# Row sums of the conditioning in the first block's feed-forward part: halved loads, a quarter of the products on GpSimd and ScalarE, folds a chunk later

## The chip, the cores and the metric

The kernel runs on one core of a Trainium2 chip. The metric is the device time of one execution in microseconds (us); the kernel before takes 3891.92 us, the median of three runs. The core's engines run side by side, each through its own instructions in a fixed order: TensorE (PE, matrix products; PEld is its loading of weights), VectorE (DVE), ScalarE (ACT), GpSimd (POOL). SyncE (SP) issues the loads from memory, one after the other. An instruction that waits for another engine or for a load holds up all that stands behind it on its engine.

## The reference, cut to what matters

The reference runs two network blocks. In the first, each of two layers is steered by numbers that come from a conditioning vector `c` (for 512 latent positions) and `c_ctx` (for 256 context positions): shift, scale and gate of the mixer and of the feed-forward part, six times 1024 numbers.

```
s_lat = silu(c);  s_ctx = silu(c_ctx)
m_lat = split(s_lat @ w_ada[li] + b_ada[li], 6)      # [1024] @ [1024, 6144]
m_ctx = split(s_ctx @ w_ada[li] + b_ada[li], 6)
...
h = rms_norm(x, g_ffn[li]) * (1 + m_lat[4]) + m_lat[3]
x = x + m_lat[5] * conv_ffn(h, ...)                  # up, 3-tap conv, silu * , down
ctx = ctx + m_ctx[5] * conv_ffn(hc, ...)             # in layer 0 only
```

The change touches the products with `w_ada` that are needed late: the last eighth of layer 0 (`m[5]`) and all six parts of layer 1. The kernel computes them while the feed-forward part of layer 0 runs.

## The kernel before

Activations lie feature by feature (128 partitions) with 768 positions in the free direction. A product at full precision is made of three TensorE products of rounded halves: every weight is loaded by SP into a buffer `wraw` (L255), rounded on ACT (`whi`, L262), its rest is taken on DVE (`wlo`, L265), and `mm3` (L271 to L273) multiplies.

`ffn` of layer 0 works in three groups of 8, 7 and 7 chunks (`GROUPS`). In an **up phase** each chunk has two products (m = 0 and 1) into four PSUM banks, which are used in turn; DVE takes them out (`zr`, L633), the convolution goes over ACT (`z`, L642) and DVE (L649), the gate over ACT and DVE (`th`, L653, L654) and GpSimd (`th`, L655), and `split` makes `gh` (ACT, L278) and `gl` (DVE, L279). Since a chunk's product of m = 0 goes into the banks of the chunk before, it can begin only when `zr` of that chunk has been taken out. In the **down phase** behind it eight products f = 0 to 7 run into `psS`, and DVE adds each to the residual (`x`, L591). I call the phases up1, down1, up2, down2, up3 and down3. Behind down3 comes layer 1: its first product (`psP` from `xh`, `xl`), a product for the shift (`psO` from `bh`, `bl`), the mean of squares (`meanrs`, L313), the inverse root on DVE, and `along` (L322), which spreads it.

The generator `rest` (`adarows`) does the conditioning beside this. It has 56 rows, in seven sets of eight; a row is 128 times 1024 numbers of `w_ada`. Before, a row is one load of 512 KB into the only buffer `rada` (L478), and four row sums on DVE (L481, each a product with the conditioning `cr` and a sum, called a dot below; its product is thrown into a `zr` buffer), into `racc`. Behind a set's last row two small TensorE products with `fold` (L486) add the two halves of the partitions, and `biased` (`mc`, `am`) adds the bias. `ffn` draws one row for each up chunk, and one or two for each f (twelve for each down phase). A scheduler then sets the order on every engine by priority, so rows can stand some instructions ahead of or behind the place where the code draws them.

Of the kernel before, what the change touches and what calls it, by code (L numbers as in the profile page):

```python
# [24 lines left out]
F32 = mybir.dt.float32  # L25
F32R = mybir.dt.float32r
I32 = mybir.dt.int32
AF = mybir.ActivationFunctionType
OP = mybir.AluOpType
# [12 lines left out]
GSTART = (0, 8, 15)  # L42
# [44 lines left out]
def drain(steps):  # L87
    for _ in steps:
        pass
# [325 lines left out]
class First(Net):  # L415
# [41 lines left out]
    def adarows(self, wk, sets):  # L457

        nc, I = self.nc, self.I
        cr = wk.tile([128, 2, 512], F32, name="cr")
        src = I["crow"]
        for h in range(2):
            nc.sync.dma_start(cr[64 * h:64 * h + 64], bass.AP(tensor=src.tensor, offset=src.offset + h * 1024, ap=[[0, 64], [1, 1024]]))
        junk = lambda: wk.tile([128, self.wide], F32, name="zr", tag="zr", bufs=2)[:, :512]
        for i in range(2):
            t = junk()
            nc.scalar.activation(t, cr[:, i, :], AF.Tanh, scale=0.5)
            nc.vector.scalar_tensor_tensor(cr[:, i, :], t, 1.0, cr[:, i, :], op0=OP.add, op1=OP.mult)  # L470
        nc.vector.tensor_scalar(cr, cr, 0.5, None, op0=OP.mult)
        fold = wk.tile([128, 64], F32, name="fold")
        nc.vector.tensor_tensor(fold, self.ident[:, 0:64], self.ident[:, 64:128], op=OP.add)
        for l, j0, n in sets:
            acc = wk.tile([128, 2, n, 2], F32, name="racc", tag="racc", bufs=2)
            for j in range(n):
                w = wk.tile([128, 2, 512], F32, name="rada", tag="rada", bufs=1)
                nc.sync.dma_start(w, I["wrow"][l, j0 + j])  # L478
                for b in range(2):
                    for i in range(2):  # L480
                        nc.vector.tensor_tensor_reduce(junk(), w[:, b, :], cr[:, i, :], 1.0, 0.0, OP.mult, OP.add, acc[:, b, j, i:i + 1])  # L481
                if j < n - 1:
                    yield
            ps = self.psT()[:, 0:2 * n]
            for b in range(2):
                nc.tensor.matmul(ps[64 * b:64 * b + 64], lhsT=fold, rhs=acc[:, b].rearrange("p j i -> p (j i)"), start=True, stop=True)  # L486
            self.biased(l, ps.rearrange("p (j i) -> p j i", i=2), j0, n)
            yield

    def run(self):  # L490
        nc, tc, I = self.nc, self.tc, self.I
        self.block("1", NT)
        self.xopen("0", I["x"])
        self.cols = []
        for l in range(DEPTH):
            c = self.cst.tile([128, 245], F32, name=f"cols{l}")
            nc.sync.dma_start(c, I["cols1"][l])
            self.cols.append(c)
        cc = self.cst.tile([128, 8, 2], F32, name="cc")
        nc.sync.dma_start(cc, I["c"])  # L500
        self.sc = self.cst.tile([128, 8, 32], F32, name="sc")
        nc.vector.memset(self.sc, 0.0)
        sc = self.sc[:, :, 0:2]
        nc.scalar.activation(sc, cc, AF.Tanh, scale=0.5)
        nc.vector.scalar_tensor_tensor(sc, sc, 1.0, cc, op0=OP.add, op1=OP.mult)
        nc.vector.tensor_scalar(sc, sc, 0.5, None, op0=OP.mult)
        self.nmx2 = self.cst.tile([128, 8], F32, name="nmx2")
        nc.sync.dma_start(self.nmx2, I["cols2"][0][:, 0:8])
        per = lambda n, k: [self.cst.tile([128, k, 2], F32, name=f"{n}{l}") for l in range(DEPTH)]
        self.mc, self.am, self.af = per("mc", 48), per("am", 8), per("af", 8)  # L510
        self.blk2 = self.cst.tile([128, 2], F32, name="blk2")
        nc.vector.memset(self.blk2, 0.0)
        nc.vector.memset(self.blk2[0:64, 0:1], 1.0)
        nc.vector.memset(self.blk2[64:128, 1:2], 1.0)
        rope = self.cst.tile([128, 2, 128], F32, name="rope")
        nc.sync.dma_start(rope, I["rope1"])
        self.rope = rope
        for l in range(DEPTH):
            self.layer(l, self.mc[l], self.am[l], self.af[l])
# [75 lines left out]
    def ffn(self, E, up, down, cw, nq, same, resid, after):  # L595

        nc, tc = self.nc, self.tc
# [5 lines left out]
        with tc.tile_pool(name="ff", bufs=1, reuse_waits="tile") as wk:  # L603
# [10 lines left out]
            rest = self.adarows(wk, ((0, 40, 8), (1, 8, 8), (1, 0, 8), (1, 16, 8), (1, 24, 8), (1, 32, 8), (1, 40, 8))) if nq > SEQ else iter(())  # L614
            held = 16 if nq > SEQ else 19
            off = 0
            for n, i0 in zip(GROUPS, GSTART):
                gv = []
                for i in range(i0, i0 + n):
                    w = self.chunk(up[i])  # L620
                    z = []
                    for m in range(2):
                        ps = [self.psP()[:, :sz + 2 * (same and j > 0)] for j, (s, sz, o) in enumerate(cuts)]
# [26 lines left out]
                        a = d[:, 1:wide - 1]  # L650
# [6 lines left out]
                    gl = wk.tile([128, wide - 2], F32R, name="gl", tag="gv", bufs=held)  # L657
                    self.split(gh, gl, th)
                    gv.append((gh, gl))
                    next(rest, None)  # L660
                if i0 == GSTART[-1]:
                    N = after(lambda: wk.tile([128, nq], F32, name="nq", tag="th", bufs=2))
                def products(ps, w, j):
# [4 lines left out]

                hold = []
                for f in range(KD):  # L670
                    for _ in range(1 + f % 2):
                        next(rest, None)
                    sz = 128 * n * 128
                    w = self.wload(down[off:off + sz].rearrange("(p a) -> p a", p=128), n, 128)
                    off += sz
                    ps = self.psS()
                    if f == KD - 1 and i0 == GSTART[-1] and N.tail is not None:
                        for s, o in ((0, 0), (256, 512)):
                            for j in range(n):
                                self.mm3(ps[:, o:o + 256], (w[0][:, j, :], w[1][:, j, :]),  # L680
                                         (gv[j][0][:, s:s + 256], gv[j][1][:, s:s + 256]), j == 0, j == n - 1)
                            x = self.xt[f][:, s:s + 256]
                            nc.vector.tensor_tensor(x, x, ps[:, o:o + 256], op=OP.add)
                            N.tail(s)
                        continue
                    for j in range(n - 1 if f < 2 else n):
                        products(ps, w, j)
                    hold.append((f, ps, w))
                    if f == 0:
                        continue  # L690
                    for g, ps, w in hold:
                        if g < 2:
                            products(ps, w, n - 1)
                        resid(g, ps)
                        if i0 == GSTART[-1]:
                            N.step(g)
                    hold = []
            drain(rest)
            self.E = N
            self.banks(("P0", "P1"), ("T0",))  # L700

# [1368 lines left out]
```

## Time and profile before

| | before |
|---|---|
| median of three runs | 3891.92 us (3887.2 to 3895.46) |
| the profiled execution | 3885.17 us |
| its span on the core | 3883.4 us |
| TensorE (PE) busy | 3663.2 us, 94% |
| VectorE (DVE) busy | 2520.5 us, 65% |
| ScalarE (ACT) busy | 1533.8 us, 39% |
| GpSimd (POOL) busy | 553.4 us, 14% |
| row sums L481 | 224 instructions, 175.2 us busy |
| loads of rows L478 | 56, 512 KB each |

The span is the stretch that the profiler recorded; the execution's time is 1.8 us longer. The six phases lie at about 492 to 1073 us of the span, up1 to 630, down1 to 704, up2 to 824, down2 to 887, up3 to 1012 and down3 to 1073. All times below are places in the span or durations.

### The profile page before, as it was taken

Reading aid. Unit: us, or ns where it says so; the run is one execution under the profiler, and the core shown is the slowest. Engines: PE = TensorE matmul, PEld = TensorE weight load, DVE = VectorE, ACT = ScalarE, POOL = GpSimd, SP = SyncE. Lnnn points to the kernel's source line nnn. Section 1 sums busy time; section 2 is a strip of 40 time slices with the busy share of each in tenths; the row PEclk is TensorE's granted clock in tenths of the full one; section 3 lists DMA queues with packets and bytes.
Section 4 is the critical chain, followed back from the end, with each engine's and each line's share of the span. In section 5 each row is a group of like instructions: output and inputs, shape, how many; then the busy total and the mean of one; then the engine's idle time right before and its main releaser. Section 6 shows DMA issues by size and latency. Waiting matters only on the chain. (4 is left out here: it accounts for less than half of the span.)

```text
span 3883.4 us, 58927 instructions
## 1 busy us (share of the span) xinstructions
PE 3663.2 (94%) x23425; PEld 2993.4 (77%) x23425; DVE 2520.5 (65%) x4866; ACT 1533.8 (39%) x2414; POOL 553.4 (14%) x381
## 2 busy tenths in 40 slices
PE   7988999999989899999999899999999988999998
PEld 5866788888887679998876676788887766778886
DVE  5567577778875657557685654656667666456555
ACT  3367432222335644334454322433344533334333
POOL 0022000000222200002112112000021221120002
PEclk9999999999999999999999999999999999999999
DMA  5233233333432133333324336322233343453232
GB/s 180 93 98 109 70 93 114 111 112 110 138 102 58 31 103 90 95 93 116 107 93 132 114 101 226 113 93 94 93 109 109 98 142 101 157 193 96 92 97 77
DMA packets 181987, 422.57 MB, mean 109 GB/s; under 512 B 42320, under 2 KB 62800, under 8 KB 181712
## 3 DMA queue, kind: packets, MB, share of 16 engines
q1 hardware_dynamic: 181712, 418.81, 34.7%
q8 instruction: 184, 3.01, 0.3%
q14 instruction: 91, 0.75, 0.1%
HBM read 373.91 MB, written 44.83 MB: 108 GB/s over the span
## 5 line engine op out<-in xcount | busy, mean ns | idle before, releaser
L262 ACT ACTIVATE whi<-wraw 128x1024 fp32r<-128x1024 f32 (+2 forms) x489 | 510.8, 1046 | 823.1 <-PE psS L272 356.8
L271 PE MATMUL psP<-xh,whi 128*128 128x512 f32 (+1 forms) x2112 | 714.9, 339 | 4.3 <-DVE zr L633 4.3
L273 PE MATMUL psP<-xh,wlo 128*128 128x512 f32 (+1 forms) x2112 | 716.2, 339 | 0.0
L272 PE MATMUL psP<-xl,whi 128*128 128x512 f32 (+1 forms) x2112 | 716.0, 339 | 0.0
L265 DVE TENSOR_TENSOR wlo<-wraw,whi 128x1024 fp32r<-128x1024 f32 (+2 forms) x471 | 575.1, 1223 | 198.2 <-ACT whi L262 190.7
L271 PEld LDWEIGHTS psP<-xh,whi 128*128 128x128 f32 x2112 | 398.7, 189 | 51.8 <-issue 4.5
L272 PEld LDWEIGHTS psP<-xl,whi 128*128 128x128 f32 x2112 | 398.9, 189 | 47.8
L273 PEld LDWEIGHTS psP<-xh,wlo 128*128 128x128 f32 x2112 | 398.8, 189 | 46.6
L655 POOL TENSOR_TENSOR th<-th,z 128x512 f32<-128x512 f32 (+1 forms) x88 | 112.7, 1280 | 1781.5 <-DVE z L649 1686.6
L271 PE MATMUL psS<-gh,whi 128*128 128x512 f32 (+1 forms) x887 | 329.8, 372 | 4.5 <-DVE x L591 3.2
L271 PE MATMUL psP<-hh,whi 128*128 128x512 f32 x800 | 327.8, 410 | 2.0 <-ACT whi L262 1.0
L273 PE MATMUL psS<-gh,wlo 128*128 128x512 f32 (+1 forms) x887 | 329.3, 371 | 0.0
L272 PE MATMUL psS<-gl,whi 128*128 128x512 f32 (+1 forms) x887 | 329.1, 371 | 0.0
L273 PE MATMUL psP<-hh,wlo 128*128 128x512 f32 x800 | 326.5, 409 | 0.7 <-DVE wlo L265 0.7
L272 PE MATMUL psP<-hl,whi 128*128 128x512 f32 x800 | 321.9, 403 | 0.0
L271 PE MATMUL psP<-whi,hh 128*128 128x256 f32 (+1 forms) x944 | 277.0, 294 | 19.0 <-ACT nk L247 4.2
L272 PE MATMUL psP<-wlo,hh 128*128 128x256 f32 (+1 forms) x944 | 273.0, 290 | 5.9 <-DVE wlo L265 5.2
L273 PE MATMUL psP<-whi,hl 128*128 128x256 f32 (+1 forms) x944 | 271.6, 289 | 1.1 <-DVE hl L362 1.1
L271 PEld LDWEIGHTS psP<-whi,hh 128*128 128x128 f32 x944 | 182.8, 194 | 29.5 <-ACT nk L247 4.8
L481 DVE CUSTOM_DVE_ANT_0 zr<-rada,cr 128x512 f32<-128x512 f32 x224 | 175.2, 824 | 45.7 <-DMA rada<-in_wrow_dram 45.1
L271 PEld LDWEIGHTS psS<-gh,whi 128*128 128x128 f32 x887 | 166.7, 188 | 39.8 <-DVE x L591 5.4
L649 DVE SCALAR_TENSOR_TENSOR z<-zr,cols,z 128x770 f32<-128x770 f32 (+3 forms) x176 | 144.3, 820 | 79.6 <-ACT z L642 44.9
(536 smaller groups left out, 6842.1 us busy)
## 6 DMA issues: line engine op xcount, KB each, us to landing
wraw<-in_up_dram SPq DMA_DIRECT2D x176, 512.0 KB
rada<-in_wrow_dram SPq DMA_DIRECT2D x56, 512.0 KB
wraw<-in_down_dram SPq DMA_DIRECT2D x64, 448.0 KB
wraw<-in_gate_dram SPq DMA_DIRECT2D x48, 512.0 KB
wraw<-in_win_dram SPq DMA_DIRECT2D x36, 512.0 KB
wraw<-in_wout_dram SPq DMA_DIRECT2D x32, 512.0 KB
wraw<-in_down_dram SPq DMA_DIRECT2D x32, 512.0 KB
wraw<-in_rwz_dram SPq DMA_DIRECT2D x28, 512.0 KB
```

Source lines behind the costliest of these rows:

```text
L262: self.nc.scalar.activation(hi[:, :n], t[:, :n], AF.Copy)
L265: (self.nc.gpsimd if self.low[self.lows % len(self.low)] == "P" else self.nc.vector).tensor_tensor(lo[:, :n], t[:, :n], hi.bitcast(F32)[:, ...
L271: mm(out, lhsT=l[0], rhs=r[0], start=start, stop=False)
L272: mm(out, lhsT=l[0], rhs=r[1], start=False, stop=False)
L273: mm(out, lhsT=l[1], rhs=r[0], start=False, stop=stop)
L481: nc.vector.tensor_tensor_reduce(junk(), w[:, b, :], cr[:, i, :], 1.0, 0.0, OP.mult, OP.add, acc[:, b, j, i:i + 1])
L649: nc.vector.scalar_tensor_tensor(d[:, o], e[:, q], c(j), d[:, o], op0=OP.mult, op1=OP.add)
L655: nc.gpsimd.tensor_tensor(th, th, z[1], op=OP.mult)
```

## The change

A row is loaded in two halves of 256 KB (`b` = 0 and 1), each a tile `rada` of its own with two buffers in turn, so that the halves `b` = 0 always use one of them and the halves `b` = 1 the other. Three of a row's four dots stay on DVE. The fourth (`b` = 1, `i` = 1) becomes a product on GpSimd, in place in the half's buffer, and a sum on ScalarE (`accum_out`), also in place. `racc` has four buffers and not two. The folds are no longer emitted behind a set: they are collected, and `folded` emits them after the next up chunk's `split` and after the last down phase, into a half of `psS` and not into `T0`. Rows are drawn once for each up chunk (twice at chunks 3 and 12), twice for each f in down1 and down2 (sixteen for each), and not at all in down3. So rows 0 to 8 fall in up1, 9 to 24 in down1, 25 to 32 in up2, 33 to 48 in down2 and 49 to 55 in up3.

```diff
         for l, j0, n in sets:
-            acc = wk.tile([128, 2, n, 2], F32, name="racc", tag="racc", bufs=2)
+            acc = wk.tile([128, 2, n, 2], F32, name="racc", tag="racc", bufs=4)
             for j in range(n):
-                w = wk.tile([128, 2, 512], F32, name="rada", tag="rada", bufs=1)
-                nc.sync.dma_start(w, I["wrow"][l, j0 + j])
                 for b in range(2):
+                    w = wk.tile([128, 512], F32, name="rada", tag="rada", bufs=2)
+                    nc.sync.dma_start(w, I["wrow"][l, j0 + j, :, b, :])
                     for i in range(2):
-                        nc.vector.tensor_tensor_reduce(junk(), w[:, b, :], cr[:, i, :], 1.0, 0.0, OP.mult, OP.add, acc[:, b, j, i:i + 1])
-                if j < n - 1:
-                    yield
-            ps = self.psT()[:, 0:2 * n]
+                        a = acc[:, b, j, i:i + 1]
+                        if b and i:
+                            nc.gpsimd.tensor_tensor(w, w, cr[:, i, :], op=OP.mult)
+                            nc.scalar.activation(w, w, AF.Copy, accum_out=a)
+                        else:
+                            nc.vector.tensor_tensor_reduce(junk(), w, cr[:, i, :], 1.0, 0.0, OP.mult, OP.add, a)
+                if j == n - 1:
+                    self.summed.append((l, j0, n, acc, fold))
+                yield
+
+    def folded(self):
+
+        for l, j0, n, acc, fold in self.summed:
+            ps = self.psS()[:, 0:2 * n]
             for b in range(2):
-                nc.tensor.matmul(ps[64 * b:64 * b + 64], lhsT=fold, rhs=acc[:, b].rearrange("p j i -> p (j i)"), start=True, stop=True)
+                self.nc.tensor.matmul(ps[64 * b:64 * b + 64], lhsT=fold, rhs=acc[:, b].rearrange("p j i -> p (j i)"), start=True, stop=True)
             self.biased(l, ps.rearrange("p (j i) -> p j i", i=2), j0, n)
-            yield
+        self.summed = []
...
                     gv.append((gh, gl))
-                    next(rest, None)
+                    self.folded()
+                    for _ in range(2 if i in (3, 12) else 1):
+                        next(rest, None)
...
                 for f in range(KD):
-                    for _ in range(1 + f % 2):
+                    for _ in range(2 if i0 != GSTART[-1] else 0):
                         next(rest, None)
...
             drain(rest)
+            self.folded()
```

Lines of the changed kernel stand some numbers higher: `zr` L633 is L644 there, `z` L642 is L653, `x` L591 is L602, the dot L481 is L486, and L483 and L484 are the new product and sum.

On SP, in down1, the loads of rows stood between loads of weights (`wraw`), each waiting for the dots of the row before it (DVE) on the only buffer:

```order
151 L478 DMA rada<-in_wrow_dram 128x1024 [waits DMAHW5_49,DVE_49]
152 L255 DMA wraw<-in_up_dram 128x1024 [waits DMAHW3_49,DVE_49]
153 L478 DMA rada<-in_wrow_dram 128x1024 [waits DMAHW7_49,DVE_49]
154 L255 DMA wraw<-in_up_dram 128x1024 [waits DMAHW6_49,DVE_49]
155 L478 DMA rada<-in_wrow_dram 128x1024 [waits DMAHW1_49,DVE_49]
```

In the changed kernel, in down1 and before the weights of the next up phase, they stand so:

```order
189 L479 DMA rada<-in_wrow_dram 128x512 [waits DMAHW6_49,Activation_49]
190 L479 DMA rada<-in_wrow_dram 128x512 [waits DMAHW4_49,DVE_49]
191 L479 DMA rada<-in_wrow_dram 128x512 [waits DMAHW0_49,Activation_49]
192 L479 DMA rada<-in_wrow_dram 128x512 [waits DMAHW7_49,DMAHW1_49,DVE_49]
193 L479 DMA rada<-in_wrow_dram 128x512 [waits Activation_49]
194 L255 DMA wraw<-in_up_dram 128x1024 [waits DMAHW3_49,DVE_49]
```

Every second load is now that of a half `b` = 1, and it waits for ACT: for the sum L484 of the row before, which reads the same buffer.

On DVE, at the end of down1 of the changed kernel, the last residual of the phase (`x`, L602) and the last weight are followed by seven dots, and only then by the first `zr` of the next up phase. A dot that waits for a load names a DMAHW queue:

```order
895 L602 SCALAR_TENSOR_TENSOR x_4324<-psS,mc_124,x_4324 128x256
896 L265 TENSOR_TENSOR wlo<-wraw,whi 128x1024 [waits DMAHW5_49,Activation_49]
897 L486 ISA zr,racc<-rada,cr 128x512 [waits DMAHW3_49,DVE_49]
898 L486 ISA racc 128x1
899 L486 ISA zr,racc<-rada,cr 128x512 [waits DMAHW4_49,DVE_49]
...
907 L486 ISA zr,racc<-rada,cr 128x512 [waits DVE_49]
...
909 L486 ISA zr,racc<-rada,cr 128x512 [waits DMAHW0_49,DVE_49]
...
911 L644 TENSOR_TENSOR zr<-psP,r 128x512 [waits DVE_49,PE_49]
```

Before, the same place had eight dots (two rows, each with one load) behind the first half of that residual:

```order
904 L591 SCALAR_TENSOR_TENSOR x_4324<-psS,mc_124,x_4324 128x512 [waits PE_49]
905 L481 ISA zr,racc<-rada,cr 128x512 [waits DMAHW0_49,DVE_49]
...
913 L591 SCALAR_TENSOR_TENSOR x_4324<-psS,mc_124,x_4324 128x256
914 L265 TENSOR_TENSOR wlo<-wraw,whi 128x1024 [waits DMAHW5_49,Activation_49]
915 L481 ISA zr,racc<-rada,cr 128x512 [waits DMAHW1_49,DVE_49]
...
921 L481 ISA zr,racc<-rada,cr 128x512 [waits DVE_49]
...
923 L633 TENSOR_TENSOR zr<-psP,r 128x512 [waits DVE_49,PE_49]
```

In both kernels all rows that the code draws in the down phase stand ahead of the next up phase's `zr`: twelve before, sixteen now.

On PE, behind the last product of layer 1's first stage, the fold and the shift's product stood ahead of the mean of squares before:

```order
5497 L273 MATMUL psP<-whi,xl 128x256
5498 L486 MATMUL psT<-racc,fold 64x16 x2
5499 L271 MATMUL psO<-whi,bh 128x256
5500 L272 MATMUL psO<-wlo,bh 128x256
...
5522 L273 MATMUL psO<-whi,bl 128x256
5523 L313 MATMUL psT<-ones,nS 128x1 x6
5524 L322 MATMUL psS<-ident,nrmy 128x128 x2
```

In the changed kernel the fold stands ahead of that stage, the mean of squares (L313) inside it, and the shift's product (`psO`) behind:

```order
5443 L496 MATMUL psS<-racc,fold 64x16 x2
5444 L271 MATMUL psP<-whi,xh 128x256
...
5477 L272 MATMUL psP<-wlo,xh 128x256
5478 L313 MATMUL psT<-ones,nS 128x1 x6
5479 L273 MATMUL psP<-whi,xl 128x256
5480 L271 MATMUL psO<-whi,bh 128x256
```

## Rows read from the trace of the kernel before

**Rows 1.** Waits, 490 to 1100 us: engine, line, waited for, total, times, longest

```profile
DVE zr L481 <- DMA rada<-in_wrow_dram: 45.1, 27, 3.8
PE psT L486 <- DVE racc L481: 9.1, 7, 2.9
PE psP L271 <- DVE zr L633: 4.3, 1, 4.3
```

**Rows 2.** Timeline, 678 to 724 us: start, duration, instruction, [idle before, releaser]

```profile
682.66 6.66 SPq L478 DMA_DIRECT2D rada<-in_wrow_dram  x2
686.43 0.69 DVE L481 CUSTOM_DVE_ANT_0 zr<-rada,cr 128x512 f32<-128x512 f32 x1 [3.79 <-DMA rada<-in_wrow_dram]
...
704.42 0.75 DVE L591 SCALAR_TENSOR_TENSOR x<-psS,mc,x 128x512 f32<-128x512 f32 x1 [2.86 <-PE psS L273]
...
711.59 0.69 DVE L481 CUSTOM_DVE_ANT_0 zr<-rada,cr 128x512 f32<-128x512 f32 x1 [2.22 <-DMA rada<-in_wrow_dram]
...
714.05 1.02 DVE L633 TENSOR_TENSOR zr<-psP,r 128x512 f32<-128x512 f32 x2
...
721.09 0.39 PE L271 MATMUL psP<-xh,whi 128*128 128x512 f32 x1
...
722.75 1.22 DVE L265 TENSOR_TENSOR wlo<-wraw,whi 128x1024 fp32r<-128x1024 f32 x1
```

**Rows 3.** Timeline: the last `gh` of up1 and up2, and the end of down2's rows

```profile
637.51 0.85 ACT L278 ACTIVATE gh<-th 128x770 fp32r<-128x770 f32 x1 [4.98 <-POOL th L655]
...
831.11 0.85 ACT L278 ACTIVATE gh<-th 128x770 fp32r<-128x770 f32 x1 [4.85 <-POOL th L655]
...
908.28 0.47 PE L271 MATMUL psP<-xh,whi 128*128 128x512 f32 x1 [4.32 <-DVE zr L633]
```

**Rows 4.** Windows behind that wait: us, engines' busy time, PEclk, DMA share, GB/s

```profile
910.00:912.00 2.00, 2.00 (x9) 1.81 (x9) 1.97 (x3) 1.31 (x3) 0.00 (x0) 0.50 0.25 102
```

**Rows 5.** Timeline of the end of an up chunk, 583 to 588 us

```profile
583.80 1.02 DVE L649 SCALAR_TENSOR_TENSOR z<-zr,hw,z 128x770 f32<-128x770 f32 x1
...
584.99 1.84 POOL L655 TENSOR_TENSOR th<-th,z 128x770 f32<-128x770 f32 x1 [15.07 <-DVE z L649]
...
585.35 2.03 DVE L481 CUSTOM_DVE_ANT_0 zr<-rada,cr 128x512 f32<-128x512 f32 x1
...
586.87 0.85 ACT L278 ACTIVATE gh<-th 128x770 fp32r<-128x770 f32 x1 [4.98 <-POOL th L655]
```

**Rows 6.** Groups by shape, whole span: count, then busy us, mean ns, idle before

```profile
L655 POOL TENSOR_TENSOR th<-th,z 128x512 f32<-128x512 f32 x66 | 72.2, 1094 | 1145.7 <-DVE z L649 1135.3 <-DVE pf L1189 10.4
L1393 POOL TENSOR_TENSOR thr<-thr 128x512 f32<-128x512 f32 x16 | 24.1, 1509 | 124.3 <-DVE thr L1358 120.4 <-issue 3.2 <-ACT whi L262 0.6
L278 ACT ACTIVATE gh<-th 128x512 fp32r<-128x512 f32 x66 | 41.7, 632 | 216.9 <-POOL th L655 216.9
L1526 ACT ACTIVATION_READ_ACCUMULATOR ae<-ae,amn 128x1 f32 x64 | 12.0, 187 | 0.0
```

**Rows 7.** Timeline: loads of 256 KB and of 192 KB and their first readers

```profile
2341.89 0.92 SPq L255 DMA_DIRECT2D wraw<-yb  x2
...
2345.09 0.63 ACT L278 ACTIVATE yu<-wraw 128x512 fp32r<-128x512 f32 x1 [3.37 <-DMA wraw<-yb]
...
2386.31 1.04 SPq L255 DMA_DIRECT2D wraw<-yb  x2
...
2388.98 0.53 ACT L278 ACTIVATE yu<-wraw 128x384 fp32r<-128x384 f32 x1 [2.56 <-DMA wraw<-yb]
```

**Rows 8.** Timeline of layer 1's beginning, 1076 to 1095 us

```profile
1076.12 0.72 ACT L281 ACTIVATE xh<-x,am 128x512 fp32r<-128x512 f32 x1 [1.60 <-DVE x L591]
...
1080.70 0.95 DVE L123 TENSOR_TENSOR nS<-nS,nq 128x768 f32<-128x768 f32 x1
...
1090.95 1.39 PE L313 MATMUL psT<-ones,nS 128*128 128x1 f32 x12
...
1094.61 1.22 PE L322 MATMUL psS<-ident,nrmy 128*128 128x128 f32 x4 [2.27 <-DVE nrmy L292]
```

More of the change, by code (lines that the diff above doesn't have):

```diff
@@ L506, in run @@
         nc.vector.tensor_scalar(sc, sc, 0.5, None, op0=OP.mult)
+        self.summed = []
         self.nmx2 = self.cst.tile([128, 8], F32, name="nmx2")
```

## Prediction

> **What bounds the kernel now.** The table of busy time puts PE at 94% of the span, so first I asked where PE is not fed during the work that the change touches. The list of waits from 490 to 1100 us has few that PE ends up paying: seven folds wait 9.1 us for row sums, and one product of up3 waits 4.3 us for `zr` [rows 1]. The reader should see that DVE waits far longer, 45.1 us in 27 waits, for loads of rows: with one buffer, a row's load can't begin before the last dot of the row before.
>
> The timeline of down1 shows this as a chain. Two loads go out between 682.66 and 689.32, the first dot of the one row stands at 686.43 (3.77 us after its load's issue), and four rows later one stands at 711.59: 6.29 us for each row, whatever PE does [rows 2]. Twelve such rows must be through before DVE may take out the first product of the next up phase (`zr`, 714.05). PE needs that only at 721.09, when it has filled the four banks with two products (16.7 us, from 704.4) [rows 2]. So after down1 the chain is hidden with 6 us to spare; after down2, whose products are shorter, it isn't, and PE begins at 908.28 after that wait of 4.3 us [rows 3]. **What counts is thus rows per down phase times time per row.**
>
> **Time per row after the change.** The halves `b` = 1 all use one buffer, and its next load waits for the ScalarE sum. One turn is:
> - landing of 256 KB. A load of this size issued at 2341.89 is read at 2345.09 (3.20), one of 192 KB at 2386.31 is read at 2388.98 (2.67) [rows 7]; the 512 KB of a row take 3.77. A straight line from 192 to 512 KB would give 2.9 for 256. I take 3.0; bounds 2.67 and 3.77.
> - the DVE dot on the half, 0.69 [rows 2].
> - from DVE's end to GpSimd's start 0.17 (583.80 + 1.02 to 584.99) [rows 5].
> - the GpSimd product 128x512: the gate's of this shape takes 1.09, another 1.51 [rows 6]. I take 1.25, nearer to the gate's, which has the same operands from SBUF.
> - GpSimd to ScalarE 0.04 (586.83 to 586.87) [rows 5].
> - the ScalarE pass 0.63, and reading its accumulator 0.19, of which I count half [rows 6].
> - 0.05 to SP, an estimate like the step above.
>
> Sum **5.9 us**; with all low ends and no accumulator read 5.3, with all high ends 7.0. That is hardly below the 6.29 of before: a chain through GpSimd and ScalarE replaces three dots of 0.69. And a down phase now has 16 rows and not 12.
>
> The Trainium skill, page "DMA: Bandwidth & Descriptors", section "Anatomy of one DMA — SWDGE (gpsimd) path", fits about 2.0 us plus bytes over 436 GB/s for one DMA, for another issue path. It would give an estimate of 2.6 us for a half and 3.2 for a row; the trace has 3.20 and 3.77, some 0.6 more, so halving saves 0.57 us by the trace as by the rule. With 2.6 the turn would be 5.5, and the sum 14 us and not 26.
>
> **down1.** The first `b` = 1 load of row 9 waits for row 8's sum: `gh` of chunk 7 ends at 638.36 [rows 3], then a GpSimd product, the step to ScalarE and a sum: 639.7. Row 24, the sixteenth, has its last dot on DVE at 639.7 + 15 x 5.9 + 3.0 + 0.7 = 731.9, then comes `zr`. PE follows about 0.8 later, behind the larger of the two pieces that take 1.02 [rows 2]: 732.7, where before it was 721.09. That is 11.6. Behind that `zr` the second weight of chunk 9 is late: from `zr` (714.05) to that weight's rest `wlo` (722.75 + 1.22) DVE took 9.9 us before [rows 2]; in the new order two more dots (1.4), two `z` of 1.02 [rows 5] and the collected folds' bias (0.4, an estimate) stand ahead of it. That is 13.7; I take 12.5, since before some of this time went into waits for ScalarE that the additions fill. Besides, `z` on ScalarE stands behind row 24's sum (639.7 + 16 x 5.9 = 734.1, 0.9 after it could begin). PE wants this weight after a quarter of a chunk pair's 16.7 us, so it went on at 725.3 before and does at 745.3 now (731.9 + 12.5 + 0.9). **Price: +20 us** at 5.9, and 16 us for each us more or less of the turn.
>
> **down2.** The last `gh` ends at 831.96 [rows 3], so the first load goes at 833.3; `zr` at 833.3 + 15 x 5.9 + 3.7 = 925.5, PE at 926.3 against 908.28. **+18 us.** Here the weights stand ahead of `zr` in the order, so nothing is added.
>
> **Clock.** Behind the wait before 908 the granted clock is 0.50 for a stretch (the level of 1.2 GHz) [rows 4]. The 2 us of that row cost 1.0, and the stretch is longer than the row; I take **1.7** for one, an estimate. down1's wait adds one.
>
> **What it gives back.** In down3 no rows stand. At the end the mean's sum `nS` waits on DVE behind a row's dots: `xh` ends at 1076.84, but `nS` runs from 1080.70; without dots it follows `xl` (0.8, an estimate) and ends at 1078.6, and the mean on PE (L313), which stood behind fold and shift product at 1090.95, can start there. In the new order the shift's 24 products fill the time of the root on DVE, so `along` comes some 4.2 after L313's start (1.4 and 24 times 0.12, an estimate; before 3.66): about 1082.9 and not 1094.61 [rows 8]. **-11.7.** Folds: seven waits make 9.1 [rows 1]; the last belongs to that end, those in down1 and down2 lie in stretches that now wait for rows, and two elsewhere give **-2**.
>
> **What costs nothing.** In up phases the GpSimd product and the sum find GpSimd idle for 15 us and ScalarE for 5 before `gh` [rows 5]; one row in 16.7 us is far from its turn. If chunks came every 6 us, it would cost as in the down phases. DVE saves 56 dots of 0.69, but a dot that starts while GpSimd works takes 2.03 and not 0.69 (585.35 beside 584.99 [rows 5]); each GpSimd product can cost DVE 0.6 to 0.8 so, which eats what is saved. Two `racc` more and `psS` for folds wait for nothing.
>
> Sum: 20 + 18 + 1.7 - 11.7 - 2 = **+26 us** on 3885.17, the profiled execution, which lies 6.75 below the median: **3918** on the median. The slope is 31 us for each us of turn. With 5.3 it is +7, with 7.0 +60.
>
> **Rivals.**
> - Faster: the turn is short enough to hide behind PE. The break-even is 5.06 us (5.9 - 26/31); below 4.75 both phases' waits are gone and only the gains are left, about -13, **3879**. For it: PE's own time allows 16 rows at that pace, and loads here might land faster than the rows of a busier stretch. Against: the lowest rows give 5.3, and ScalarE and DVE work in order, so a sum or a dot also stands behind weights.
> - No change: a turn of 4.8 to 5.3, loss and gain cancel, **3892**.
> - Worse: GpSimd is held up by DVE. The Trainium skill, page "SBUF — State Buffer", section "Who interferes with whom", has DVE and GpSimd share a port pair that goes wholly to whoever comes first, when DVE has two inputs in SBUF. As a mechanism of this kernel: a dot (0.69) or a `wlo` (1.22) runs when the product comes up, and the turn is 6.6 or more: **+48, 3940**. For it: the dot of 2.03. Against: the gate's product starts at 584.99 while a dot is under way, and takes 1.84 for 770 columns, where 1.09 for 512 would give 1.65 [rows 5, 6]: 0.2 late, not 0.7.
>
> **How the numbers follow.** My forecast (turn 5.3 to 6.5) 0.60, worse 0.14, no change 0.12, faster 0.14. What a measurement tells from no change is about 0.2%, 7.8 us. Slower by more is forecast and worse, 0.74; within it 0.12; faster 0.14. The range reaches from 3888, in the middle of no change, to 3945, a little under what all high ends give; about 0.2 is left out.
>
> **What would show it.** The distance of `rada` loads for `b` = 1 in down1: 5.9 us. PE's `psP` L271 waits for `zr` (L644) once after down1 and once after down2, for 10 to 20 us each, with SP's row loads waiting for ScalarE (L484). GpSimd product 1.1 to 1.5, longer dots beside it. L313 of layer 1 starts 4 us after the last residual, and PE has no fold wait. I am wrong if those PE waits are missing or short, that is, if rows run at 5 us or less, or if `zr` doesn't wait for the last row.

## The result and the profile after

The changed kernel takes **3919.52 us** (3912.68 to 3925.86, four runs) against 3889.56 us of before with its later runs (3882.87 to 3895.46): a ratio of 1.0077, 95% interval 1.0052 to 1.0103. It is slower, by 30 us, and 3918 had been forecast. The profiled execution has a span of 3920.8 us, 37.4 above that of before, and a mean granted clock of 0.975 (before 0.982).

Where the time went shows in the places of the phases: the first product of each phase on PE, and the first product of `along` (L322) in layer 1. The table is made from these starts in the two traces.

| stretch | before, us | after, us | difference | forecast |
|---|---|---|---|---|
| up1 | 138.3 | 138.6 | +0.3 | 0 |
| down1 and up2 | 193.7 | 213.3 | **+19.6** | +20 |
| down2 and up3 | 188.2 | 217.0 | **+28.8** | +18 |
| down3 | 61.3 | 60.0 | -1.4 | in -2 of the folds |
| layer 1 to `along` | 21.2 | 8.5 | **-12.7** | -11.7 |
| together | 602.8 | 637.3 | +34.6 | +26 with clock and folds |

The list of waits of the changed kernel from 490 to 1140 us (total, times, longest) has these rows where before had [rows 1]:

```profile
DVE zr L486 <- DMA rada<-in_wrow_dram: 72.4, 42, 4.3
PE psS L271 <- DVE x L602: 19.4, 6, 6.9
PE psS L496 <- DVE racc L486: 12.8, 1, 12.8
PE psS L496 <- ACT rada L484: 12.3, 2, 6.4
PE psP L271 <- DVE zr L644: 7.5, 2, 3.8
```

PE now waits for row sums, first in the folds (L496), which stand ahead of the next chunk, and then in that chunk's product. On PE's timeline each wait has its place behind a down phase; the last two rows are the end of layer 1's first stage:

```profile
737.21 0.40 PE L496 MATMUL psS<-racc,fold 128*64 128x16 f32 x2 [5.89 <-ACT rada L484]
741.43 0.80 PE L271 MATMUL psP<-xh,whi 128*128 128x512 f32 x1 [3.82 <-DVE zr L644]
...
946.86 0.40 PE L496 MATMUL psS<-racc,fold 128*64 128x16 f32 x2 [12.78 <-DVE racc L486]
953.63 0.40 PE L496 MATMUL psS<-racc,fold 128*64 128x16 f32 x2 [6.37 <-ACT rada L484]
957.71 0.79 PE L271 MATMUL psP<-xh,whi 128*128 128x512 f32 x1 [3.68 <-DVE zr L644]
...
1125.76 1.39 PE L313 MATMUL psT<-ones,nS 128*128 128x1 f32 x12
1130.01 0.61 PE L322 MATMUL psS<-ident,nrmy 128*128 128x128 f32 x4
```

Ten and twenty-three us of waiting stand before 741.43 and 957.71. The folds of the last whole set (rows 16 to 23 behind down1, rows 40 to 47 behind down2) wait for that set's last sums, and the next product waits for `zr`, which stands on DVE behind the dots of row 24 or 48. So the list names three releasers, but they are one thing: the rows of the phase, one after the other.

This is the last turn but one of that chain in down1, put together from the timelines of SP, DVE, GpSimd and ScalarE:

```profile
731.20 12.09 SPq L479 DMA_DIRECT2D rada<-in_wrow_dram  x5
734.30 0.69 DVE L486 CUSTOM_DVE_ANT_0 zr<-rada,cr 128x512 f32<-128x512 f32 x1 [3.33 <-DMA rada<-in_wrow_dram]
735.14 1.26 POOL L483 TENSOR_TENSOR rada<-rada,cr 128x512 f32<-128x512 f32 x1 [4.72 <-DVE racc L486]
736.43 0.63 ACT L484 ACTIVATE rada<-rada 128x512 f32<-128x512 f32 x1 [5.26 <-POOL rada L483]
736.97 0.19 ACT L484 ACTIVATION_READ_ACCUMULATOR rada<-rada 128x1 f32 x1
740.07 0.69 DVE L486 CUSTOM_DVE_ANT_0 zr<-rada,cr 128x512 f32<-128x512 f32 x1 [2.50 <-DMA rada<-in_wrow_dram]
740.69 1.02 DVE L644 TENSOR_TENSOR zr<-psP,r 128x512 f32<-128x512 f32 x2
```

From the load's issue at 731.20 to its dot are 3.10 us, then 0.69 and 0.15, GpSimd 1.26, 0.03, ScalarE to the end of its accumulator read at 737.16. The next load's dot begins at 740.07, and `zr` stands right behind that last dot. The next load of that half went out at 737.18, so this turn is 6.0 us; the shortest in down1, from one sum L484 to the next, was 5.33. Over down1 sixteen turns took 100.1 us (sum L484 of row 8 at 642.10, of row 24 at 742.21), **6.26 us each**; over down2 102.4 us (856.12 to 958.48), **6.40 each**. The forecast had 5.9. SP's list says whom the loads waited for:

```profile
SPq L479 <- ACT rada L484: 201.3, 48, 6.0
SPq L479 <- DVE racc L486: 73.1, 33, 7.7
```

From the issue of the load to its dot the 32 turns of down1 and down2 took 2.60 to 4.50 us, on average 3.18 in down1 and 3.26 in down2, and in all but one of them DVE sat idle before that dot until the load was there. The Trainium skill, page "DMA: Bandwidth & Descriptors", section "Anatomy of one DMA — SWDGE (gpsimd) path", would give an estimate of 2.6 us for such a load, by a fit for another issue path. These loads took more, so the trace decides.

### The profile page after: what moved, and what is told of

It is laid out like the page before. It is cut to its first block, busy times and chain, and to the rows that moved or that the text cites. A ratio compares the mean times of both kernels' runs of the same rounds, so it can differ in the third digit from the quotient of the medians.

```text
span 3920.8 us, 59220 instructions
## 1 busy us (share of the span) xinstructions
PE 3671.2 (94%) x23425; PEld 3002.5 (77%) x23425; DVE 2496.3 (64%) x4754; ACT 1569.3 (40%) x2526; POOL 631.0 (16%) x437
## 5 line engine op out<-in xcount | busy, mean ns | idle before, releaser
L271 PE MATMUL psS<-gh,whi 128*128 128x512 f32 (+1 forms) x887 | 333.1, 375 | 20.9 <-DVE x L602 19.6
L272 PEld LDWEIGHTS psP<-wlo,hh 128*128 128x128 f32 x944 | 183.9, 195 | 12.6 <-DVE wlo L265 8.9
```

Source lines behind the costliest of these rows:

```text
L271: mm(out, lhsT=l[0], rhs=r[0], start=start, stop=False)
L272: mm(out, lhsT=l[0], rhs=r[1], start=False, stop=False)
```

## The experiments

Theory A is that of the prediction: rows of a down phase, one turn each, must be through before the next up phase, so PE waits for turns times rows. Rivals: B, GpSimd's products hold up DVE; C, the late folds, which now stand ahead of the next chunk on PE, make the wait. All runs are against the kernel before on the same chip; its medians beside them were 3890.4 to 3891.44 us, so a difference between two runs of different rounds is good to a us or two beside their own scatter. "Region" below is the stretch from the first product of up1 to `along` in the profiled execution (602.8 before, 637.3 after); it leaves out the rest of the program, which differs by some us from run to run (up1 begins between 484.7 and 493.8 us in the fourteen traces).

**Three buffers (e1_bufs3).**

```diff
-                    w = wk.tile([128, 512], F32, name="rada", tag="rada", bufs=2)
+                    w = wk.tile([128, 512], F32, name="rada", tag="rada", bufs=3)
```

> The changed kernel with three rada buffers and not two, all else kept (draws, GpSimd product, ScalarE sum, late folds in psS). Theory A (a chain of load, dot, product and sum on one buffer, 6.3 us for each row, times 16 rows per down phase, holds up the next up phase): with three buffers a load runs while the half before it is worked on, a row takes about 4.2 us, 16 rows 67 us, both phases hide them, and only the gains are left: 3872 to 3882 us, 8 to 18 us under the kernel before. Theory B (GpSimd products hold up DVE, which is then too slow for rows and weights together): the buffers change little, 3910 to 3920. Theory C (the folds, now in psS and ahead of the next chunk on PE, make PE wait): 3910 to 3920 as well, with the fold waits kept.

3873.31 us, ratio 0.9944 (0.9922 to 0.9966), region 587.1. One number turned 30 us of loss into 17 of gain, with GpSimd, ScalarE, draws and folds as they were: as A had said, and neither B nor C. The row's turn in down1 fell to 3.96 us (sums L484 at 641.25 and, sixteen later, 704.63). Of its waits two rows matter:

```profile
DVE zr L486 <- DMA rada<-in_wrow_dram: 22.1, 24, 2.1
PE psS L271 <- DVE x L602: 10.0, 3, 5.2
```

DVE's waits for loads fell from 72.4 to 22.1 us, and PE waits no longer for folds. What is left is a wait that I had not foreseen, and that the changed kernel has too (19.4 us in six waits): for residuals of a down phase, the first above all, which stands on DVE behind the dots of the first rows.

**All four dots on DVE (e2_dve).**

```diff
-                        if b and i:
-                            nc.gpsimd.tensor_tensor(w, w, cr[:, i, :], op=OP.mult)
-                            nc.scalar.activation(w, w, AF.Copy, accum_out=a)
-                        else:
-                            nc.vector.tensor_tensor_reduce(junk(), w, cr[:, i, :], 1.0, 0.0, OP.mult, OP.add, a)
+                        nc.vector.tensor_tensor_reduce(junk(), w, cr[:, i, :], 1.0, 0.0, OP.mult, OP.add, a)
```

> The changed kernel with the fourth dot back on DVE: no GpSimd product and no ScalarE sum, still half loads in two buffers and 16, 16 and 0 rows in the down phases. Theory A: a half's buffer is free again after landing 3.1 and two dots 1.3, a row takes about 4.6 us and 16 take 74, so down1 hides them and down2 nearly: 3872 to 3885 us. Theory B says the same, for another reason (no GpSimd beside DVE). Theory C: fold waits stay, 3900 to 3920.

3873.27 us, 0.9949 (0.9928 to 0.9969), region 587.0. The turn is 4.86 us in down1 and 4.78 in down2 (from the last dot of row 8 to that of row 24, and of row 32 to row 48), where 4.6 was worked out. So the quarter on GpSimd and ScalarE lengthened the chain by some 1.5 us a row and bought nothing that PE needed. B had said the same of this run, so it does not tell A from B; e1 and e4 do.

**Twelve rows in each down phase (e3_twelve).**

```diff
-                    for _ in range(2 if i0 != GSTART[-1] else 0):
+                    for _ in range(1 + f % 2):
```

> The changed kernel with the draws of before in the down phases (12 for each, so down3 has the last 8 rows). Theory A: 12 turns of 6.3 us end at about 716 us after down1 (PE wants them at 721) and at about 910 after down2 (908 before), so the loss goes and about 10 us of the gains stay: 3876 to 3888 us. Theory B: each row still costs DVE the same, only spread out: 3895 to 3910. Theory C: 3900 to 3920, since the folds stand where they stood.

3891.19 us, 0.9998 (0.9982 to 1.0013), region 605.2: 28 us below the changed kernel, but some 3 to 15 above what A said. The waits behind down1 and down2 are gone as A said; instead:

```profile
PE psS L271 <- DVE x L602: 22.7, 7, 7.1
```

Seven waits for residuals on DVE; the longest stands at the head of down1, and one of 5.1 us at the end of down3: there the eight late rows, at 6.7 us each, delayed the residuals, and down3 took 71.2 us and not 60.0. A row's long turn costs wherever something stands behind it on DVE, not only ahead of `zr`. A had counted one place.

**The changed draws alone on the kernel before (e4_draws).**

```diff
-                    next(rest, None)
+                    for _ in range(2 if i in (3, 12) else 1):
+                        next(rest, None)
...
-                    for _ in range(1 + f % 2):
+                    for _ in range(2 if i0 != GSTART[-1] else 0):
```

> The kernel before (whole loads of 512 KB, four dots on DVE, folds at once) with the changed draws alone: 16, 16 and 0 rows in the down phases, two at chunks 3 and 12. Theory A: the row of before takes 6.29 us too, so 16 of them end some 25 us later after down1 (PE waits 18) and after down2 (PE waits 25), and the end gains 12: 3910 to 3925 us, as slow as the changed kernel, without GpSimd, ScalarE, halves or late folds. Theories B and C: nothing that they blame is in it, so 3875 to 3892.

3929.54 us, 1.0092 (1.0071 to 1.0113), region 638.7: by the region as slow as the whole change (637.3), by the median 10 us slower and 5 above what A had said, without GpSimd, ScalarE, halves or late folds. Its waits on PE:

```profile
PE psT L486 <- DVE racc L481: 49.3, 10, 24.3
```

The longest (24.3) is behind down2, the next (16.7) behind down1, where 25 and 18 were expected.

**The folds of before in the changed kernel (e5_folds)** and **late folds alone on the kernel before (e8_latefolds).**

```diff
                 if j == n - 1:
                     self.summed.append((l, j0, n, acc, fold))
+                    self.folded()
                 yield
...
-            ps = self.psS()[:, 0:2 * n]
+            ps = self.psT()[:, 0:2 * n]
...
-                    self.folded()
...
-            self.folded()
```

> The changed kernel with the folds of before: emitted when a set's last row is drawn, into T0. Theory A: PE's waits after the down phases are set by when rows are through, whichever instruction stands first behind them, so the time stays with the changed kernel's: 3912 to 3928 us. Theory C (late folds in psS, ahead of the next chunk on PE, cause the waits): most of the loss goes, 3885 to 3900.

3933.31 us, 1.0113 (1.0095 to 1.0131), region 644.2: slower than the changed kernel, and 5 us above what A had said. In e8_latefolds the edit is that part of the change's diff by itself (`racc`, `summed`, `folded`), with a second row at chunk 3:

```diff
-                    next(rest, None)
+                    self.folded()
+                    for _ in range(2 if i == 3 else 1):
+                        next(rest, None)
```

> The kernel before with the late folds alone (collected, psS, four racc; one row more at chunk 3, so that the first set is whole in time). Theory A: the folds' waits in the down phases and at the end go, nothing else changes: 2 to 5 us faster, 3885 to 3889. Theory C: 10 us or more slower, 3900 or above.

3877.8 us, 0.9965 (0.9951 to 0.9978), region 595.4. C falls twice: with early folds the changed kernel is slower still, and late folds alone are a gain. A had put that gain at 2 to 5 us; the median says 13 and the region 7.4 (of the two profiled executions 3.2 us more lie ahead of the region and 3.4 behind it, where no fold is). Late folds are worth 6.9 us of the region in the changed kernel and 7.4 in the kernel before. Of the 7.4, 4.0 lie at layer 1's beginning, where L313 and `along` now stand:

```profile
1079.31 1.39 PE L313 MATMUL psT<-ones,nS 128*128 128x1 f32 x12
1084.07 0.68 PE L322 MATMUL psS<-ident,nrmy 128*128 128x128 f32 x4 [0.24 <-DVE nrmy L292]
```

The layer begins at 1066.83 in that trace, so `along` comes 17.2 us later and not 21.2 [rows 8]; the rest is a bit over 1 us in down1 and in down3 and less elsewhere.

**Rows behind the residuals, three buffers (e6_behind), the same with all dots on DVE (e7_behind_dve), and fewer rows at a phase's head (e11_later).**

```diff
-                    for _ in range(2 if i in (3, 12) else 1):
+                    for _ in range(2 if i in (3, 5, 7, 9, 12, 14) else 1):
...
-                    for _ in range(2 if i0 != GSTART[-1] else 0):
-                        next(rest, None)
...
                             N.step(g)
                     hold = []
+                    for _ in range(2 if i0 != GSTART[-1] else 0):
+                        next(rest, None)
```

> Three buffers as in e1_bufs3, and rows drawn behind the residuals of a down phase (2 for each f from 1, 14 for each phase) with doubles at chunks 3, 5, 7, 9, 12 and 14. What e1 left was that PE waits some 5 us in each down phase for the first residual, which stands on DVE behind dots that wait for loads. If that is dots ahead of the residual, fewer dots there shorten it by 1 to 3 us a phase: 3866 to 3873 us. If it comes from DVE's load as a whole, no gain: 3873 to 3878.

3872.61 us, 0.9955 (0.9941 to 0.997), region 586.5: no gain over e1. PE's waits for the first residual are 6.7 and 3.9 us (5.2 and 4.7 in e1): behind the last `gl` of up1 the scheduler still put eight dots ahead of that residual, where e1 has ten, so moving the draw in the code hardly moved the dots. The edit did not do what it was for.

The second, e7_behind_dve, is e6 with the edit of e2:

```diff
-                        if b and i:
...
-                        else:
...
+                        nc.vector.tensor_tensor_reduce(junk(), w, cr[:, i, :], 1.0, 0.0, OP.mult, OP.add, a)
```

> As e6_behind, with all four dots on DVE. Theory A: with three buffers the row's time isn't the bound, so the GpSimd product is worth nothing by itself: within 5 us of e6, 3866 to 3878. Theory B (GpSimd holds up DVE): 5 to 10 us below e6. If DVE is short of time in up phases, as a GpSimd product would be meant to mend: 5 to 15 us above e6.

3863.9 us, 0.9934 (0.9917 to 0.9952), region 577.4, the fastest of all. Against e6 the medians differ by 8.7 us and the regions by 9.1, though the two intervals overlap slightly. The row's turn is 3.6 us (4.2 in e6); PE's waits for the first residual are 2.1 and 2.3 us, though twelve dots stand ahead of it in down1 and not eight. The groups by shape from 490 to 1140 us, first those of e7, then of e6:

```profile
L482 DVE CUSTOM_DVE_ANT_0 zr<-rada,cr 128x512 f32<-128x512 f32 x224 | 172.9, 812 | 5.0 <-DMA rada<-in_wrow_dram 4.8
```

```profile
L486 DVE CUSTOM_DVE_ANT_0 zr<-rada,cr 128x512 f32<-128x512 f32 x168 | 138.1, 847 | 22.6 <-DMA rada<-in_wrow_dram 22.5
L483 POOL TENSOR_TENSOR rada<-rada,cr 128x512 f32<-128x512 f32 x56 | 81.4, 1453 | 92.6 <-DVE racc L486 92.6
```

GpSimd took 35 us of work off DVE, and DVE waited 18 us more for loads. What I had put under A, a difference within 5 us, did not come; 5 to 10 us below e6 is what I had put under B. The rows show something of both: the dots lengthened from 812 to 847 ns beside GpSimd, 6 us over all of them, and the waits for loads, 18 us, fit a buffer that is held longer. No run separates the two. It looks as if the length of a row's turn counts where it stands ahead of a residual, even with three buffers, and DVE's busy time less.

The third, e11_later, has this edit on e7:

```diff
-                    for _ in range(2 if i in (3, 5, 7, 9, 12, 14) else 1):
+                    for _ in range(2 if i in (2, 3, 4, 5, 7, 9, 11, 13, 16, 19) else 1):
...
-                    for _ in range(2 if i0 != GSTART[-1] else 0):
+                    for _ in range(2 if f > 1 and i0 != GSTART[-1] else 0):
```

> e7_behind_dve with fewer dots at the head of a down phase: rows only for f from 2 (12 for each phase), and ten double chunks in the up phases. If e7's two waits of 2.2 and 2.5 us for the first residual come from dots ahead of it, they go, and the clock with them: 3856 to 3862 us. If up phases have no DVE time left for second rows, it is slower than e7: 3866 to 3876.

3864.97 us, 0.9944 (0.9929 to 0.9958), region 580.5: not told apart from e7, where 3856 to 3862 was expected. The waits for the first residual stayed (4.2 and 2.2 us): twelve dots still stand ahead of it in the order. What sets that order in the scheduler stays open.

**Fourteen rows in each down phase, two buffers (e9_fourteen).**

```diff
-                    for _ in range(2 if i in (3, 12) else 1):
+                    for _ in range(2 if i in (2, 3, 5, 9, 11, 12) else 1):
...
-                    for _ in range(2 if i0 != GSTART[-1] else 0):
+                    for _ in range(2 if f and i0 != GSTART[-1] else 0):
```

> The changed kernel with 14 rows in down1 and in down2 and not 16 (none at f = 0; doubles at chunks 2, 3, 5, 9, 11 and 12 take the other four), all else kept, two buffers too. Theory A: two turns fewer in each phase, so each wait behind it shrinks by two of the turns that the changed kernel's trace shows (6.26 and 6.40 us), 25 us in all: about 3895 us, 3888 to 3902. If something else holds PE up behind the down phases (folds, GpSimd beside DVE), the rows' number matters little: 3910 to 3920.

3913.14 us, 1.0057 (1.0044 to 1.007), region 624.6: 12.7 us off the region, 6.4 off the median, and not 25. In the one half of the region it came out: down2 and up3 took 203.5 us, 13.4 less than in the changed kernel, two turns. In the other the rows came back: down1 and up2 won 4.1 only, up1 lost 4.8. The list of waits says how:

```profile
PE psP L271 <- DVE zr L644: 10.2, 7, 3.8
```

Seven waits for `zr`, where the changed kernel had two. Three of them, of 1.6 to 1.9 us, end at 614.23, 768.63 and 805.81, each between the sums of the two rows of a double: the second row's dots stand ahead of that chunk's `zr` too. At chunk 3 of the changed kernel such a row had cost nothing, but three of them in one up phase are too many while a turn is that long.

**Clearing down3 when a row is short (e10_dve_twelve):** the edit of e3 on e2_dve.

```diff
-                    for _ in range(2 if i0 != GSTART[-1] else 0):
+                    for _ in range(1 + f % 2):
```

> e2_dve (half loads, late folds, all dots on DVE) with 12 rows in each down phase, so that the last 8 stand in down3. It prices the clearing of down3 when a row is short. Theory A: the rows of down3 end well before the last residuals, the end of down3 loses at most a few us against e2: 3872 to 3880 us. If rows in down3 cost what they cost in the kernel before (about 12 us at layer 1's beginning): 3882 to 3888.

3870.42 us, 0.9953 (0.9941 to 0.9966), region 585.8, within 1.2 us of e2's. Eight rows in down3 cost 4.9 us there (64.9 against 60.0), and down2 and up3, with four rows fewer, give 6.4 back. With a short turn it no longer matters much where rows stand.

**ScalarE out of the turn (e12_apart).**

```diff
-                            nc.gpsimd.tensor_tensor(w, w, cr[:, i, :], op=OP.mult)
-                            nc.scalar.activation(w, w, AF.Copy, accum_out=a)
+                            p = wk.tile([128, 512], F32, name="radp", tag="radp", bufs=1)
+                            nc.gpsimd.tensor_tensor(p, w, cr[:, i, :], op=OP.mult)
+                            nc.scalar.activation(p, p, AF.Copy, accum_out=a)
```

> The changed kernel with one link taken out of the turn: GpSimd writes its product into a tile of its own, so the half's buffer is free when GpSimd has read it, and no longer waits for the ScalarE sum (0.63 and the read of the accumulator, some 0.75 us of the turn). 16, 16 and 0 rows and two buffers as in the changed kernel. Theory A: 0.75 us off each of 16 turns, 12 us off each phase, 24 in all: about 3896 us, 3888 to 3904. Against it: if a row's time is set by what its instructions wait for on DVE (dots behind weights and residuals) and not by the chain on the buffer, nothing changes: 3912 to 3922.

3896.03 us, 1.0018 (1.0006 to 1.003), region 610.2: 23.5 us below the changed kernel (27.1 by the region), 24 had been worked out. Turns are 5.50 us in down1 and 5.12 in down2 (0.76 and 1.28 less). The loads wait for DVE and GpSimd now:

```profile
SPq L479 <- DVE racc L487: 165.1, 110, 8.8
...
SPq L479 <- POOL radp L484: 13.3, 12, 1.1
```

But the edit took out two links and not one. In the changed kernel GpSimd's product, which writes into the half's buffer, waits for the DVE dot that reads it; with a tile of its own it waits for the load alone, as the groups of the changed kernel (490 to 1140 us) and of this run (484 to 1105) show:

```profile
L483 POOL TENSOR_TENSOR rada<-rada,cr 128x512 f32<-128x512 f32 x56 | 81.7, 1459 | 177.9 <-DVE racc L486 173.5 <-DMA rada<-in_wrow_dram 4.4
```

```profile
L484 POOL TENSOR_TENSOR radp<-rada,cr 128x512 f32<-128x512 f32 x56 | 89.2, 1593 | 167.1 <-DMA rada<-in_wrow_dram 166.5 <-DVE cr L471 0.6
```

The gain is not even either. Down2 and up3 fell by 21.1 us, about sixteen times the 1.28 of the turn; down1 and up2 by 6.1 only, since PE had no more than 9.7 us of waiting there to lose, 0.9 of it stayed, and 3.9 us of waits for the next chunk's weights came up instead. So a shorter turn gives its time back where PE waits for it, which is A; that 24 came out is in part luck.

## Why the prediction was right, point by point

- **What bounds: rows per down phase times a row's turn.** Shown: more buffers (e1), a shorter turn (e2, e12) and fewer rows (e3) each take 23 us or more off the changed kernel, and e4 has the whole loss from the draws alone. Fewer rows help only where the rows taken out cost less elsewhere: e9 took off 6.4.
- **The turn, 5.9 us.** The mechanism was right, the size low: 6.26 and 6.40. In the turn shown above every step agrees with its term to 0.1 us, and the whole is 5.98. On average two terms were too small. The load to its dot took 3.18 us in down1 and 3.26 in down2 where I had 3.0, and GpSimd's product 1.48 and 1.47 where I had 1.25: in 15 of the 32 rows it took 1.36 to 2.12, when a dot or a `wlo` was still under way as it began, and 1.26 to 1.29 in the others. All other steps together are within 0.1 us of their terms, and the sum on ScalarE began 0.03 us behind the product in every row, so it did not stand behind other work. Why some loads took up to 4.5 us stays open.
- **down1, +20.** 19.6 was measured, but from other parts. The first load came 2 us later: the prediction's 639.7 is short by its own terms, since 638.36 with a product, a step and a sum (1.25, 0.04 and 0.63) is 640.3. The turns took 5.4 more. The 8.4 that I had put on the second weight of chunk 9 (and on `z` behind row 24's sum) did not occur: PE has no wait over 0.5 us between 741.43 and the next down phase. The `wlo` on DVE right behind the first `zr`, at 741.88, must be that weight's; I had taken a later one for it. Two errors met, and that the number came out is luck.
- **down2, +18.** Measured 28.8: the term that was mis-sized. Turns of 6.40 for 5.9 make 7.5 us, the later first load 2.8 (856.87, 12.3 us into the phase, where 833.3 is 9.5 into that of before). PE began at 957.71, 28.7 us later from the phase's first product than before.
- **Waits inside the down phases.** The prediction has no term for PE's waits for residuals, 19.4 us in six, and for the longer phases that they make (down1 82.4 us for 74.1, down2 72.2 for 63.0). They are covered by the wait behind the phase: the dots of the chain waited for loads, not for residuals, so the rows and not PE set the end. In e1 and e3 they come to light.
- **The signs.** PE was to wait for `zr` once behind each phase, for 10 to 20 us, and not for folds. It waited 9.7 and 22.8 us, most of it in folds (25.1) and the rest for `zr` (7.5): the folds now stand ahead of that product, and the prediction had them wait for nothing.
- **Clock, +1.7.** The term was for the wait behind down1. There, once PE worked again at 741.43, the granted clock was 0.50 up to 744 us and 0.83 in the 2 us behind, which by these windows costs 1.6 us, an estimate:

```profile
742.00:744.00 2.00, 2.00 (x8) 1.68 (x7) 1.26 (x1) 1.79 (x4) 0.17 (x1) 0.50 0.03 7
744.00:746.00 2.00, 2.00 (x11) 1.73 (x10) 1.80 (x2) 1.08 (x2) 0.00 (x0) 0.83 0.85 249
...
957.70:959.70 2.00, 2.00 (x6) 1.71 (x7) 1.67 (x8) 1.22 (x3) 0.75 (x1) 0.50 0.00 0
```

  Behind 957.71 it was 0.50 for 4 us; before had such a stretch there too [rows 4]. The size of the term was not tested by itself.
- **The end, -11.7.** Measured -12.7, with `along` 4.25 us behind L313 (4.2 forecast). The clearing of down3 is enough for it: e4, which has the folds of before, has 8.5 us there too, and so has e5. Late folds alone (e8) give 4.0 of it; the two do not add up.
- **Folds, -2 beside that.** Too small: between e5 and the changed kernel late folds give 6.9 us of the region, none of it at the end; 4.9 lie in up1.
- **What costs nothing.** In single up chunks right (up1 +0.3). For DVE wrong: I had GpSimd's products eat what the missing dots save. From 490 to 1140 us the dots kept DVE busy for 140.2 us and not 175.2; 56 dots at e2's 0.778 (174.2 us busy over 224) would be 43.6, so about a fifth is lost on balance. A single product did cost DVE what I had said or more: 28 dots took 1.25 to 1.81 us beside one, which lengthened them by some 26 us in all. But e2 has 21 dots over 0.75 us as well, and the changed kernel only one other.

The rivals: "faster" needed a turn under 5.06. e1 and e2 (4.0 and 4.8) lie below it and are 17 us faster, where the gains alone had been put at 13. e12 lies nearest: at 5.50 and 5.12 it is still 4.6 us slower than before by the median, 7.4 by the region, and the prediction's slope gives 7 for 5.3. That fits a break-even of about 5, but no run stands at it. "Worse" by GpSimd held up came true in part: its product took 1.26 to 2.27 us, mean 1.46, which is 0.2 us of a turn and not the 0.7 of that rival, and the dots beside it up to 1.81 instead of 0.69. The Trainium skill, page "SBUF — State Buffer", section "Who interferes with whom", has a DVE instruction with two inputs in SBUF contend with a GpSimd instruction that reads SBUF; the trace agrees, by the lengths just given. The lengthened dots are those of the next half, which the chain does not wait for, so they cost little. The groups of the changed kernel (least, median and longest in ns):

```profile
L486 DVE CUSTOM_DVE_ANT_0 zr<-rada,cr x168: 678/691/2032, 521.2 to 1066.7; 128x512 f32<-128x512 f32 x168
L483 POOL TENSOR_TENSOR rada<-rada,cr x56: 1261/1293/2273, 524.1 to 1068.7; 128x512 f32<-128x512 f32 x56
L484 ACT ACTIVATE rada<-rada x56: 629/633/637, 525.4 to 1070.1; 128x512 f32<-128x512 f32 x56
```

The sum of the region, +34.6 in one execution, is 8.6 over the forecast's 26; that the median came within 1.5 us of 3918 is in part luck: the rest of the program varies by some us, and the medians differ by 30 us where the two profiled executions differ by 37.4. In the profiled execution the stretch behind `along` was 2.0 us longer than before.

Open: whether the halves by themselves gain, since no run had them with the draws of before and the folds of before; what lengthens some loads of a half; and which of the scheduler's priorities puts dots ahead of a phase's first residual.

## What to carry to other kernels

Work that hides beside an engine still has its own serial chain: load, each engine that reads the buffer, release. Multiply its turn by the number of turns that stand ahead of something the busy engine needs, and compare with that engine's time there; only then decide where to put it. Moving a step to an idle engine can lengthen the turn though it lightens the loaded engine; a buffer more (e1) or links fewer (e12) shorten it, and here one `bufs=3` was worth 46 us.

## What was not expected of the hardware

GpSimd's 128x512 product of two tiles in SBUF took 1.46 us on average, against 1.09 for the gate's product of the same shape [rows 6]. Neighbours on DVE make a part of it: the median is 1.29, and a product at 708.79 with nothing beside it on DVE took 1.29 too. Writing in place does not make the rest, since the gate's product does so as well and the product of e12, which doesn't, took 1.28 at least. What does was not tried.
